# Weight splits of an up-projection asked for one step earlier, and rows of x loaded one by one

## The chip, the core and the metric

The kernel runs on one core of a Trainium2 chip. TensorE (PE) does the matrix products, ScalarE (ACT), VectorE (DVE) and GpSimd (POOL) work beside it, and SyncE (SP) asks for most of the DMA transfers. The metric is the device time of one execution in microseconds (us), as a median of several. Three runs before the change gave 2205.82, 2207.04 and 2207.34 us.

## The reference

One layer of a hybrid encoder works on 2048 prompt tokens and 64 sample tokens of 1024 channels. The first half (normalised input, a combined projection, a pooling mixer, a chunked matrix memory, an output projection) is not touched by the change. The second half is a gated MLP with a causal convolution of width 3 over the tokens:

```python
h2 = rmsnorm(x, g2) * (1 + sc2) + sh2
up = h2 @ w_up                                   # 1024 -> 2 * 2816
upp = jnp.concatenate([conv_buf, up], 1)
conv = b_conv + sum(w_conv[j] * upp[:, j:j + T] for j in range(3))
a, g = jnp.split(conv, 2, -1)
x = x + gt2 * ((jax.nn.silu(g) * a) @ w_down)    # 2816 -> 1024
y = rmsnorm(x, g_final)
```

All of it is f32, and the products have to be as exact as three passes make them: each operand is kept as a high half (rounded to the type that PE multiplies) and a low half (what is left), and a product is high times high, high times low and low times high.

## The kernel before the change

**Groups, parts, pairs.** The MLP works on the 2112 tokens in three groups (`o.g` 0, 1, 2) of 704 tokens each. The 22 pairs of column blocks of `w_up` (block f of `a` and block f of `g`, 128 columns each) are taken in parts: 5, 5, 6 and 6 pairs in groups 0 and 1, and 6, 4, 4, 4 and 4 in group 2. Behind each part stands a down part, which multiplies the part's results with rows of `w_down` and adds them to the rows of x.

**Products.** A pair's two column blocks are computed by a scheme of Winograd's kind: seven products in place of eight, each of 12 matmuls of 352 columns (4 blocks of the inner dimension, 3 passes), with sums of weights and sums of inputs prepared earlier. `Pair.products` (the part of the code around L1575 to L1650) emits in this order: B11, B21, then the last product T4 of the pair before, then T2, T3, B22 and T1. The function `product` (L1539) emits one of them: it calls `pump()`, takes a weight unit with `get_unit()`, and emits its 12 matmuls (L1546). Between two products stand steps on ACT and DVE for this pair and the pair before, called in the program `rest(...)`:

- `copy_u4` (L1625, ACT) copies the sum left by T1 from PSUM, and `sum_g1` and `sum_a` (L1555, DVE) add it to two others.
- `self.s1` (L1593, ACT) is copied after B11, and `ea` (L1605, DVE) is its sum with B21's result. It reads the PSUM bank in which B22 later starts, so B22 has to wait for it. `sum_g0` is `eg` at L1555.
- `scale_a` and `scale_g` (L1529, ACT; tiles `ta` and `tg`) begin the convolution, `taps_a` and `taps_g` (L1534, DVE) finish it. Then come `silu` (L1656, ACT), `gate` (L1663, DVE) and the split of the result into halves `av` (L1682, ACT, and L1692, DVE).

**Weight units.** All weights come through one stream of units in the order of their use. A unit of `w_up` or `w_down` is loaded into a `raw` tile (L368, four of them) and split into a `wt` tile (six of them, taken in turn): the high half by ACT (L384), then the low half by DVE (L387). A unit of sums (`wsum`, L376) is loaded straight into a `wt` tile and split there; a unit that was split and stored by group 0 (`wsplit`, L373) is loaded whole and needs no split. In groups 1 and 2 a pair takes three raw units (for B11, B21 and T4), two of sums (for T3 and B22) and two whole ones (for T2 and T1); in group 0 four are of sums, and two of these are stored with L392. The unit for B22 is called the B22 sum below, the one for T3 the T3 sum.

**pump.** `pump()` looks at the first four units that wait for their use: it emits both halves of the split for the first three and only ACT's high half for the fourth. Then it asks for loads while fewer than seven units wait and fewer than six `wt` tiles are in use (`live[0]`), and `product` takes one from that count after its matmuls. So a unit's high half stands on ACT three products ahead of its use, and its low half on DVE two products ahead.

**What sets the order.** On PE, ACT, DVE and POOL the order is the one in which the program emits (a manual schedule). On SP a scheduler sets the order of the DMA requests; SP works them off one after the other, and a request that waits for a free tile holds up those behind it.

**Rows of x.** In the last step of a down part, `down_end` (L2072), the result of each of the eight rows is added to a row of x, which `load_x2` (L1867) fetches. In group 0 two rows are asked for after each pair. In group 1 three rows are asked for after the last pair of the first part, and the other five in one go before that part's down part (L2037). In group 2 the rows come another way.

Of the kernel before, what the change touches and what calls it, by code (L numbers as in the profile page):

```python
# [18 lines left out]
KD = D // P  # L19
# [9 lines left out]
NE = 3  # L29
# [33 lines left out]
def tile_layer(ctx: ExitStack, tc: tile.TileContext, xT, vecs, cst, rst, rowv, w_mod, w_ada, w_qkou, w_v, w_pool,  # L63
# [12 lines left out]
    def bank(nm, shape=(P, 512)):  # L76
        q = turn[nm]
        q.append(q.pop(0))
        return q[-1].tile(list(shape), F32, tag="bank", name=nm)
# [3 lines left out]
    def mm_ps():  # L83
        return bank("mm")
# [18 lines left out]
    def tick(i=0):  # L103
        q = bg[i]
        while q:
            try:
                next(q[0])
                return
            except StopIteration:
                q.pop(0)  # L110
# [130 lines left out]
    for g in range(NG):  # L241
        o = Grp()
# [118 lines left out]
    def issue():  # L361
        u = Unit()
        src, u.n, place, u.keep, u.stays = stream[pos[0]] + (OUT, None, False)[len(stream[pos[0]]) - 2:]
        u.at = pos[0]
        if place == OUT:
            u.raw = raw_tile()
            to = u.raw[:, :u.n]
            nc.sync.dma_start(out=to if len(src.shape) == 2 else to.rearrange("p (s c) -> p s c", s=2), in_=src)  # L368
        else:
            u.w = wt_tile(u.n)  # L370
            if place == WHOLE:
                u.state = 2
                nc.sync.dma_start(out=u.w.bitcast(F32)[:, :, :u.n], in_=src)  # L373
            else:
                u.raw = u.w.bitcast(F32)[:, 1]
                nc.sync.dma_start(out=u.raw[:, :u.n], in_=src)  # L376
        pos[0] += 1
        pend.append(u)

    def work_out(u, upto=2):  # L380
        if u.state == 0 and upto > 0:
            if u.w is None:
                u.w = u.home()
            act.activation(u.w[:, 0, :u.n], u.raw[:, :u.n], AF.Copy)  # L384
            u.state = 1
        if u.state == 1 and upto > 1:
            dve.tensor_tensor(out=u.w[:, 1, :u.n], in0=u.raw[:, :u.n], in1=u.w[:, 0, :u.n].bitcast(F32), op=ALU.subtract)  # L387
            u.state = 2
# [5 lines left out]
    def pump():  # L394

        while True:
            for i, u in enumerate(pend[:ahead[1]]):
                if u.w is not None or live[0] < ahead[2] or u.stays:
                    work_out(u, 2 if i < ahead[1] - ahead[3] else 1)
            if (pos[0] >= len(stream) or len(pend) >= ahead[0] or live[0] >= ahead[2]  # L400
                    or sum(u.w is None for u in pend) >= RB
                    or pos[0] < n_att and sum(u.w is not None for u in pend) >= WB - 2):
                break
            issue()

    def get_unit():
        if not pend:
            issue()
        u = pend.pop(0)
        work_out(u)  # L410
        keep(u)
        return u.w
# [218 lines left out]
    for g in range(NFG):  # L631
        o = Grp()
# [868 lines left out]
    def do(n=1):  # L1501

        for _ in range(n):
            if todo:
                todo.pop(0)()

    def both_of(a, b):
        return lambda: (a(), b())
# [32 lines left out]
    def product(ps, Bo, nm, first):  # L1541
        pump()
        U = get_unit()
        for kc in range(4):
            for pi, (a, b) in enumerate(PASSES):
                pe.matmul(ps[:, :FH], U[:, a, kc * P:(kc + 1) * P], Bo.at(nm, kc, b),  # L1546
                          start=(first and kc == 0 and pi == 0), stop=(kc == 3 and pi == 2), skip_group_check=not first)
            if kc % 2:
                tick(0)
        tick(5)  # L1550
        live[0] -= 1

    def plus(o, half, ext, u, ps):
        for (a, b, d) in spans(o, half):
            dve.tensor_tensor(out=ext[:, d:d + b - a], in0=ps[:, a:b], in1=u[:, a:b], op=ALU.add)  # L1555
# [4 lines left out]
    class Pair:  # L1560
# [10 lines left out]
        def products(self, old):  # L1571
# [12 lines left out]
            def extra(i):  # L1584
                for at, step in self.more:
                    if at == i:
                        step()
            rest((old, Pair.copy_u4), (older, Pair.gate))
            product(b1, Bo, "B11", True)
            rest((old, Pair.sum_g1), (old, Pair.sum_a))  # L1590
            extra(0)
            self.s1 = half_tile("s1")
            act.activation(self.s1, b1[:, :FH], AF.Copy)  # L1593
            rest((older, Pair.split_hi))
            product(b2, Bo, "B21", True)
            rest((old, Pair.scale_a), (older, Pair.split_lo))
            extra(1)
# [263 lines left out]
    def load_x2(o, ks=range(KD)):  # L1861
        x3 = []
        for k in ks:
            if k % 2 == 0:
                xp[k // 2] = f2.tile([P, 2 * FT], F32, tag=f"x{k}", name=f"x{k}")
            x = xp[k // 2][:, k % 2 * FT:(k % 2 + 1) * FT]
            got = nc.sync.dma_start(out=x, in_=x2d[k, :, o.t0:o.t0 + FT])  # L1867
            if o.g > 0:
                tc.keep_in_program_order(got)
            x3.append(x)  # L1870
        return x3
# [90 lines left out]
    x3, ssum = [], None  # L1962
    act.activation(RF[:, 0:1], V[:, 0:1], AF.Silu)
    bg[5].append(down_sums())
    for o in fgroups:
# [5 lines left out]
        for pi, (f0, f1_) in enumerate(SPARTS if o.g in SGS else PARTS):  # L1971
# [46 lines left out]
            if o.g in SGS and pi == 0:  # L2018
                Y = [f2.tile([P, 2 * FT], F32, tag=f"x{2 * m}", name=f"x{2 * m}") for m in range(4)]
                x3 = [Y[n // 2][:, n % 2 * FT:(n % 2 + 1) * FT] for n in range(KD)]  # L2020
            if o.g in SGS and not lastp:
# [11 lines left out]
                do(9)  # L2033
                held.append(pair)
                continue
            if pi == 0 and o.g > 0:
                x3 += load_x2(o, range(len(x3), KD))  # L2037
            if not o.last:
                if lastp:
                    drain(0, 1)  # L2040
# [7 lines left out]
            def down(ps, W, ks, secs, stays=False):  # L2048
                for k in ks:
                    U = W.at(k // 4)  # L2050
                    for (a, b) in PASSES:
                        for i, (lo, hi) in enumerate(secs):
                            pe.matmul(ps[i][:, :hi - lo], U[:, a, k % 4 * P:(k % 4 + 1) * P], av[k](b, lo, hi),  # L2053
                                      start=(k == 0 and (a, b) == PASSES[0]), stop=(k == nf - 1 and (a, b) == PASSES[-1]))
                    if (k % 4 == 3 or k == nf - 1) and not stays:
                        live[0] -= 1
                    pump()
                    if todo:
                        do()
                    elif o.last:  # L2060
                        tick(1 - k % 2)
                    else:
                        tick((1, 5, 5, 5)[k % 4])

            def down_end(n, ps, secs):
                while Y and n not in made:
                    next(conv)
                for i, (lo, hi) in enumerate(secs):
                    for (a, b, s) in o.segs:
                        a, b = max(a, lo), min(b, hi)  # L2070
                        if a < b:
                            dve.scalar_tensor_tensor(out=x3[n][:, a:b], in0=ps[i][:, a - lo:b - lo], scalar=gt2(n, s),  # L2072
                                                     in1=x3[n][:, a:b], op0=ALU.mult, op1=ALU.add)
                if not lastp:
                    return
                lo, hi = secs[0][0], secs[-1][1]
                if ends and n == KD - 1:
                    sq7 = fscr()
                    act.activation(sq7[:, :hi - lo], x3[n][:, lo:hi], AF.Square)
                    sums.append((sq7, lo))  # L2080
                else:
                    fsq_acc(ssum, x3[n][:, lo:hi], lo, hi, n == 0)
                if ends:
                    act.activation(x3[n][:, lo:hi], x3[n][:, lo:hi], AF.Copy, scale=V[:, V_GF + n:V_GF + n + 1])
# [7 lines left out]
            todo.extend([both_of(pair.sum_g1, old.gate), both_of(pair.sum_a, old.split_hi), both_of(old.split_lo, pair.scale_a)])  # L2092
            for n in range(NE - 1):
                pss.append([mm_ps() for _ in both])
                down(pss[n], Ws[n], range(nf - 2), both)
                if n == 0:
                    do(9)
                    pair.last_product()
                    todo.extend([both_of(pair.sum_g0, pair.scale_g), pair.taps_a, pair.taps_g, pair.silu, pair.gate,
                                 pair.split_hi, pair.split_lo])  # L2100
            for n in range(NE - 1):
                down(pss[n], Ws[n], [nf - 2], both)
            pss.append([mm_ps() for _ in both])
            down(pss[-1], Ws[-1], range(nf - 1), both)
            do(9)
            for n in range(NE):
                down(pss[n], Ws[n], [nf - 1], both)
# [2 lines left out]
            for secs in [(c,) for c in ENDS] if ends else (both,):  # L2110
                sums = [(ssum, 0)]
                for n in range(NE, KD):
                    ps = [mm_ps() for _ in secs]
                    down(ps, rows[n], range(nf), secs, ends)
                    down_end(n, ps, secs)
                if ends:
                    bg[0].append(final_end(o, x3, sums, *secs[0]))
        if not o.last:
            drain(1)
            bg[0].append(final(o, x3, ssum))  # L2120
            x3 = []
# [86 lines left out]
```

## Time and profile before

| what | value |
|---|---|
| median of three runs | 2207.04 us |
| the profiled execution's own time | 2208.67 us |
| its span in the profile | 2206.9 us |
| granted TensorE clock, mean | 0.998 |
| DVE busy | 1660.9 us, 75% of the span |
| ACT busy | 1037.7 us, 47% |
| DMA moved | 521.66 MB, mean 236 GB/s |

The profile page gives the busy time of each engine and groups of instructions by line, with the idle time of their engine just before them and what ended it. PEld is the weight load of TensorE, which runs ahead of the matmuls; its idle time is the better measure of a wait, because a matmul's end in the profile is modelled. The timeline gives instructions in order of time, equal neighbours merged into one row: start, duration, engine, line, what is written from what, how many, and in square brackets the idle time before and who ended it. "SPq" is SP's queue of requests, where the duration of a merged row reaches from the first request to the end of the last.

### The profile page before, as it was taken

What the parts mean: (1) busy time and instruction counts of PE and PEld (TensorE: products, weight loads), DVE (VectorE), ACT (ScalarE), POOL (GpSimd) and SP (SyncE); (2) the same over time, 40 slices, a digit from 0 to 9 for tenths busy, and PEclk for the clock granted to TensorE, in tenths of its full rate; (3) what the DMA queues carried; (4) which work ended last, traced back from release to release, by engine and by line L of the source; (5) the groups of instructions that cost most, each with busy time, mean ns of one, the idle gap of its engine ahead of it and who ended that gap; (6) DMA issues with size and microseconds to landing.
All of it is one profiled execution on the core that took longest, in us unless ns stands there. A gap on an engine that the chain in (4) does not pass through costs nothing. (4 is left out here: it accounts for less than half of the span.)

```text
span 2206.9 us, 38374 instructions
## 1 busy us (share of the span) xinstructions
PE 2180.6 (99%) x13708; PEld 2067.8 (94%) x13708; DVE 1660.9 (75%) x3124; ACT 1037.7 (47%) x2024; POOL 224.3 (10%) x514
## 2 busy tenths in 40 slices
PE   8999999999999999999999999999999999999998
PEld 7888888888899999999999999999999999999998
DVE  5887669577765778797958687787857597888885
ACT  4653334235243456464636444545435355555454
POOL 0010000001000100000101210000000321011112
PEclk9999999999999999999999999999999999999999
DMA  9977987997898696768667975667468665555562
GB/s 348 363 246 261 336 276 241 324 325 242 282 331 275 223 310 200 233 207 275 212 197 234 308 235 192 218 193 245 152 203 255 204 198 168 159 162 179 160 199 81
DMA packets 294975, 521.66 MB, mean 236 GB/s; under 512 B 26456, under 2 KB 115928, under 8 KB 294784
## 3 DMA queue, kind: packets, MB, share of 16 engines
q1 hardware_dynamic: 280448, 482.74, 67.2%
q10 hardware_dynamic: 11776, 28.09, 3.3%
q0 software_dynamic: 2560, 8.39, 1.0%
q8 instruction: 108, 1.77, 0.3%
q14 instruction: 83, 0.68, 0.1%
HBM read 399.97 MB, written 119.14 MB: 235 GB/s over the span
## 5 line engine op out<-in xcount | busy, mean ns | idle before, releaser
L1546 PE MATMUL mm<-hx,wt 128*128 128x352 f32 x5544 | 893.0, 322 | 5.3 <-DVE wt L387 3.7
L1546 PEld LDWEIGHTS mm<-hx,wt 128*128 128x128 f32 x5544 | 880.5, 188 | 13.1 <-DVE wt L387 9.1
L441 PE MATMUL mm<-hl,wt 128*128 128x512 f32 (+2 forms) x1920 | 395.8, 358 | 2.1 <-DMA wt<-hl_kept 2.1
L2053 PE MATMUL mm<-av,wt 128*128 128x352 f32 (+2 forms) x2400 | 386.9, 322 | 2.1 <-ACT av L1682 1.8
L2053 PEld LDWEIGHTS mm<-av,wt 128*128 128x128 f32 x2400 | 382.2, 188 | 4.3 <-ACT av L1682 2.1
L384 ACT ACTIVATE wt<-raw 128x512 fp32r<-128x512 f32 (+3 forms) x510 | 288.3, 579 | 207.3 <-PE mm L2053 60.9
L387 DVE TENSOR_TENSOR wt<-raw,wt 128x512 fp32r<-128x512 f32 (+3 forms) x510 | 323.4, 648 | 65.8 <-ACT wt L384 65.3
L441 PEld LDWEIGHTS mm<-hl,wt 128*128 128x128 f32 x1920 | 312.5, 188 | 49.6 <-issue 5.3
L441 PE MATMUL mm<-mx,wt 128*128 128x512 f32 (+1 forms) x960 | 186.5, 353 | 0.0
L441 PEld LDWEIGHTS mm<-mx,wt 128*128 128x128 f32 x960 | 158.7, 188 | 25.1 <-ACT mx L1402 1.1
L384 ACT ACTIVATE wt<-wt 128x512 fp32r<-128x512 f32 x176 | 110.3, 627 | 108.3 <-DMA wt<-wsum 101.3
L1534 DVE SCALAR_TENSOR_TENSOR tg<-eg,V,tg 128x704 f32<-128x704 f32 (+1 forms) x132 | 125.7, 952 | 33.6 <-ACT tg L1529 31.3
L387 DVE TENSOR_TENSOR wt<-wt 128x512 fp32r<-128x512 f32 x176 | 119.5, 686 | 31.0 <-ACT wt L384 30.9
L2072 DVE SCALAR_TENSOR_TENSOR x<-mm,MOD,x 128x352 f32<-128x352 f32 (+4 forms) x152 | 77.9, 559 | 75.2 <-PE mm L2053 75.2
L1534 DVE SCALAR_TENSOR_TENSOR ta<-ea,V,ta 128x704 f32<-128x704 f32 (+1 forms) x132 | 125.5, 950 | 5.9 <-ACT ta L1529 3.5
L1801 PE MATMUL mm<-av,wt 128*128 128x352 f32 x576 | 95.5, 322 | 0.0
L1801 PEld LDWEIGHTS mm<-av,wt 128*128 128x128 f32 x576 | 92.8, 188 | 0.0
L1610 ACT ACTIVATE u<-mm 128x352 f32<-128x352 f32 x66 | 30.5, 462 | 120.4 <-PE mm L1546 58.0
L206 DVE SCALAR_TENSOR_TENSOR acc<-raw,CA,acc 128x512 f32<-128x512 f32 x84 | 60.5, 745 | 32.4 <-DMA raw<-w_ada 32.3
L1656 ACT ACTIVATE tg<-tg 128x704 f32<-128x704 f32 (+1 forms) x66 | 52.3, 793 | 63.8 <-DVE tg L1534 63.7
L1555 DVE TENSOR_TENSOR eg<-mm,u 128x352 f32<-128x352 f32 x154 | 69.8, 465 | 13.2 <-ACT u L1625 9.6
L1138 PE MATMUL mm<-wt,hl 128*128 128x256 f32 (+1 forms) x576 | 70.9, 282 | 0.0
(332 smaller groups left out, 2282.7 us busy)
## 6 DMA issues: line engine op xcount, KB each, us to landing
wt<-hl_kept SPq DMA_DIRECT2D x108, 512.0 KB, 6.0
raw<-w_up SPq DMA_DIRECT2D x198, 256.0 KB, 3.9
wt<-wsum SPq DMA_DIRECT2D x176, 256.0 KB, 4.5
wt<-wsplit SPq DMA_DIRECT2D x88, 512.0 KB, 4.5
w<-w_up SPq DMA_DIRECT2D x88, 256.0 KB, 5.6
wsum<-w SPq DMA_DIRECT2D x44, 512.0 KB, 5.8
wsplit<-wt SPq DMA_DIRECT2D x44, 512.0 KB, 5.5
raw<-w_down SPq DMA_DIRECT2D x88, 256.0 KB, 4.2
```

Source lines behind the costliest of these rows:

```text
L206: dve.scalar_tensor_tensor(out=acc[s], in0=w, scalar=CA[:, k, s:s + 1], in1=acc[s], op0=ALU.mult, op1=ALU.add)
L384: act.activation(u.w[:, 0, :u.n], u.raw[:, :u.n], AF.Copy)
L387: dve.tensor_tensor(out=u.w[:, 1, :u.n], in0=u.raw[:, :u.n], in1=u.w[:, 0, :u.n].bitcast(F32), op=ALU.subtract)
L441: pe.matmul(ps[bi][:, :hi - lo], U[:, a, k % 4 * P:(k % 4 + 1) * P], mv[k][:, b, lo:hi], start=(at == 0 and pi == 0), stop=(k == order[-1] ...
L1138: pe.matmul(ps[ti][:n, :cols], h[4 * kh + k4][:, b, lo:lo + n], U[:, a, k4 % 2 * cols:(k4 % 2 + 1) * cols], start=(kh == 0 and k4 == 0 and ...
L1534: dve.scalar_tensor_tensor(out=t[:, :E], in0=ext[:, j:j + E], scalar=wc(j, f), in1=t[:, :E], op0=ALU.mult, op1=ALU.add)
L1546: pe.matmul(ps[:, :FH], U[:, a, kc * P:(kc + 1) * P], Bo.at(nm, kc, b), start=(first and kc == 0 and pi == 0), stop=(kc == 3 and pi == 2), ...
L1555: dve.tensor_tensor(out=ext[:, d:d + b - a], in0=ps[:, a:b], in1=u[:, a:b], op=ALU.add)
L1656: act.activation(self.tg[:, :E], self.tg[:, :E], AF.Silu)
L1801: pe.matmul(ps, U[:, x, w:w + P], quad.d[nm][z], start=(start and k == 0 and pi == 0), stop=(k == 1 and pi == 2), skip_group_check=not start)
L2053: pe.matmul(ps[i][:, :hi - lo], U[:, a, k % 4 * P:(k % 4 + 1) * P], av[k](b, lo, hi), start=(k == 0 and (a, b) == PASSES[0]), stop=(k == n ...
L2072: dve.scalar_tensor_tensor(out=x3[n][:, a:b], in0=ps[i][:, a - lo:b - lo], scalar=gt2(n, s), in1=x3[n][:, a:b], op0=ALU.mult, op1=ALU.add)
```

## The change

```diff
@@ product
                 tick(0)
         tick(5)
         live[0] -= 1
+        pump()
@@ the loop over groups and parts, ahead of the down part
-            if pi == 0 and o.g > 0:
-                x3 += load_x2(o, range(len(x3), KD))
+            def row(n):
+                if len(x3) <= n < KD:
+                    x3.extend(load_x2(o, range(len(x3), n + 1)))
@@ the down part (NE is 3, KD is 8)
                 pss.append([mm_ps() for _ in both])
+                row(n)
                 down(pss[n], Ws[n], range(nf - 2), both)
...
             pss.append([mm_ps() for _ in both])
+            row(NE - 1)
             down(pss[-1], Ws[-1], range(nf - 1), both)
+            row(NE)
             do(9)
...
                     ps = [mm_ps() for _ in secs]
+                    row(n + 1)
                     down(ps, rows[n], range(nf), secs, ends)
```

The first part adds a call of `pump()` behind each product. The call at the head of the next product then finds nothing left to do, so the splits and requests of one `pump()` move ahead of the steps that stand between two products. Nothing is added or taken away on PE, ACT or DVE, and PE's own order is unchanged; up to the MLP, SP's order is unchanged too. Line numbers after L1551 move by one, those after L2036 by two or more.

The second part asks for a row of x one step before it is needed. It reaches one place, the first down part of group 1, where five rows were asked for at once.

**Place 1: ACT and DVE between two pairs of group 1 (pair 18 handing over to pair 19).** In these rows `wt_18145` and `wt_18143` are the T3 sum, `wt_18183` and `wt_18178` the B22 sum, `wt_18273` and `wt_18267` the B11 weights of pair 20, `wt_18295` and `wt_18293` its B21 weights. ACT before:

```order
L1625 ACTIVATE u4_18179<-mm_18032 128x352
L1593 ACTIVATE s1_18201<-mm_18177 128x352
L1682 ACTIVATE av_18203<-tg_18121 128x352 x2
L384 ACTIVATE wt_18145<-wt_18145 128x512
L1529 ACTIVATE ta_18222<-ea_18099,V_105 128x704
L384 ACTIVATE wt_18183<-wt_18183 128x512
L1610 ACTIVATE u2_18267<-mm_18177 128x352
L1529 ACTIVATE tg_18270<-eg_18197,V_105 128x704
L384 ACTIVATE wt_18273<-raw_18228 128x512
L384 ACTIVATE wt_18295<-raw_18230 128x512
```

ACT after:

```order
L1626 ACTIVATE u4_18182<-mm_18035 128x352
L384 ACTIVATE wt_18143<-wt_18143 128x512
L1594 ACTIVATE s1_18204<-mm_18180 128x352
L1683 ACTIVATE av_18206<-tg_18125 128x352 x2
L384 ACTIVATE wt_18178<-wt_18178 128x512
L1529 ACTIVATE ta_18228<-ea_18102,V_105 128x704
L384 ACTIVATE wt_18267<-raw_18223 128x512
L1611 ACTIVATE u2_18271<-mm_18180 128x352
L1529 ACTIVATE tg_18274<-eg_18200,V_105 128x704
L384 ACTIVATE wt_18293<-raw_18225 128x512
```

Each high half has moved ahead of the steps between two products: the B22 sum's now stands ahead of the scaling `ta`, behind which it stood.

DVE before, the same stretch (`dq` is background work on sums of `w_down`):

```order
L387 TENSOR_TENSOR wt_18145<-wt_18145 128x512
L1534 SCALAR_TENSOR_TENSOR ta_18222<-ea_18099,V_105,ta_18222 128x704 x2
L1605 TENSOR_TENSOR ea_18246<-mm_18178,s1_18201 128x352
L1555 TENSOR_TENSOR eg_18197<-mm_18123,u2_18118 128x352
L387 TENSOR_TENSOR wt_18183<-wt_18183 128x512
L1780 TENSOR_TENSOR dq_18175<-dq_18175 128x128
L1781 TENSOR_TENSOR dq_18175<-dq_18175 128x128
L1783 TENSOR_TENSOR dq_18175<-dq_18175 128x128
L1784 TENSOR_TENSOR dq_18175<-dq_18175 128x128
L1534 SCALAR_TENSOR_TENSOR tg_18270<-eg_18197,V_105,tg_18270 128x704 x2
L387 TENSOR_TENSOR wt_18273<-raw_18228,wt_18273 128x512
L387 TENSOR_TENSOR wt_18295<-raw_18230,wt_18295 128x512
```

DVE after:

```order
L387 TENSOR_TENSOR wt_18178<-wt_18178 128x512
L1534 SCALAR_TENSOR_TENSOR ta_18228<-ea_18102,V_105,ta_18228 128x704 x2
L1606 TENSOR_TENSOR ea_18249<-mm_18181,s1_18204 128x352
L1556 TENSOR_TENSOR eg_18200<-mm_18127,u2_18122 128x352
L1781 TENSOR_TENSOR dq_18175<-dq_18175 128x128
L1782 TENSOR_TENSOR dq_18175<-dq_18175 128x128
L1784 TENSOR_TENSOR dq_18175<-dq_18175 128x128
L1785 TENSOR_TENSOR dq_18175<-dq_18175 128x128
L387 TENSOR_TENSOR wt_18267<-raw_18223,wt_18267 128x512
L1534 SCALAR_TENSOR_TENSOR tg_18274<-eg_18200,V_105,tg_18274 128x704 x2
L387 TENSOR_TENSOR wt_18293<-raw_18225,wt_18293 128x512
L387 TENSOR_TENSOR wt_18312<-raw_18245,wt_18312 128x512
```

The low half of the B22 sum stood behind the two sums `ea` and `eg` and now stands ahead of the taps `ta`; of the next pair's three raw low halves, one now stands ahead of the taps `tg` and two behind them.

**Place 2: SP, the request for the B22 sum of pair 20 in group 1.** Here `wt_18297` and `wt_18295` are the T3 sum of that pair, `wt_18333` and `wt_18328` its B22 sum. SP before:

```order
L373 DMA wt_18275<-wsplit_130 128x1024
L376 DMA wt_18297<-wsum_129 128x512
L368 DMA raw_18378<-w_up 128x512
L368 DMA raw_18399<-w_up 128x512
L376 DMA wt_18333<-wsum_129 128x512
```

SP after:

```order
L373 DMA wt_18269<-wsplit_130 128x1024
L368 DMA raw_18374<-w_up 128x512
L376 DMA wt_18295<-wsum_129 128x512
L368 DMA raw_18393<-w_up 128x512
L368 DMA raw_18515<-w_down 128x512
L376 DMA wt_18328<-wsum_129 128x512
```

Two raw requests still stand right ahead of the B22 sum, one unit further on in the stream than before. With four raw tiles, `raw_18393` and `raw_18515` take the tiles of `raw_18225` and `raw_18245`, so they wait for the two low halves that stand last in DVE's rows above, behind the taps `tg`.

**Place 3: SP around the first down part of group 1.** `raw_14813` before and `raw_14802` after are the same unit, the third piece of 128 columns of `w_down`; the tiles x2, x4 and x6 take rows 3 to 7 of x. SP before:

```order
L368 DMA raw_14767<-w_down 128x128
L368 DMA raw_14785<-w_down 128x128
L1867 DMA x2_14639<-x2d_132 128x704
L1867 DMA x4_14800<-x2d_132 128x704 x2
L1867 DMA x6_14803<-x2d_132 128x704 x2
L368 DMA raw_14813<-w_down 128x128
L368 DMA raw_14824<-w_down 128x512
```

SP after:

```order
L368 DMA raw_14757<-w_down 128x128
L368 DMA raw_14784<-w_down 128x128
L368 DMA raw_14802<-w_down 128x128
L1868 DMA x2_14642<-x2d_132 128x704
L1868 DMA x4_14805<-x2d_132 128x704 x2
L368 DMA raw_14821<-w_down 128x512
```

The third 128-column piece now stands ahead of the rows of x, and three rows stand there in place of five; rows 6 and 7 come later, among the first requests for the next part's `w_up`.

## The prediction, made before the changed kernel was run

> **What bounds the kernel now.** I read the page's busy times first, then the waits of TensorE, then the timeline of a quiet pair.
>
> ```profile
> span 2206.9 us, 38374 instructions
> PE 2180.6 (99%) x13708; PEld 2067.8 (94%) x13708; DVE 1660.9 (75%) x3124; ACT 1037.7 (47%) x2024; POOL 224.3 (10%) x514
> L1546 PEld LDWEIGHTS mm<-hx,wt 128*128 128x128 f32 x5544 | 880.5, 188 | 13.1 <-DVE wt L387 9.1
> PEld mm L1546 <- DVE wt L387: 9.1, 19, 0.7
> PEld mm L2053 <- ACT av L1682: 2.1, 1, 2.1
> ```
>
> PE is busy 99% of the span, and the change takes no matmul away. So it can win only what PE idles: 13.1 us in the 462 products, 9.1 us of it in 19 waits for the low half of a weight, and one wait of 2.1 us in a down part. It can lose much more, because every step between two products stands in an in-order queue that PE needs within a few us. The rhythm shows in a quiet stretch of group 1. ACT's timeline of pair 19:
>
> ```profile
> 1652.79 0.46 ACT L1625 ACTIVATE u<-mm 128x352 f32<-128x352 f32 x1 [1.01 <-PE mm L1546]
> 1654.69 0.46 ACT L1593 ACTIVATE s<-mm 128x352 f32<-128x352 f32 x1 [1.44 <-PE mm L1546]
> 1655.82 0.62 ACT L384 ACTIVATE wt<-wt 128x512 fp32r<-128x512 f32 x1
> 1656.34 0.97 ACT L1529 ACTIVATE ta<-ea,V 128x704 f32<-128x704 f32 x1
> 1658.16 0.63 ACT L384 ACTIVATE wt<-wt 128x512 fp32r<-128x512 f32 x1 [0.85 <-DMA wt<-wsum]
> 1660.48 0.47 ACT L1610 ACTIVATE u<-mm 128x352 f32<-128x352 f32 x1 [1.69 <-DVE eg L1555]
> 1660.84 0.97 ACT L1529 ACTIVATE tg<-eg,V 128x704 f32<-128x704 f32 x1
> 1666.09 0.47 ACT L1625 ACTIVATE u<-mm 128x352 f32<-128x352 f32 x1 [0.74 <-PE mm L1546]
> ```
>
> The copies at 1652.79 and 1666.09 each wait for the end of a T1, so a pair takes 13.30 us, 1.90 us for each of seven products. B22 is the sixth: PE reaches it 9.50 us after the first copy, at 1662.29 by this clock. The row at 1658.16 is the high half of the B22 sum. It waited 0.85 us for its load, behind the scaling `ta`, where the wait cost nothing.
>
> **The change part by part.**
>
> *Rows of x.* These rows are SP's, ACT's and PE's (weight load) in the first down part of group 1, and the windows around it:
>
> ```profile
> 1335.75 0.93 SPq L368 DMA_DIRECT2D raw<-w_down  x2
> 1336.73 2.52 SPq L1867 DMA_DIRECT2D x<-x2d  x5
> 1339.35 0.85 SPq L368 DMA_DIRECT2D raw<-w_down  x2
> ...
> 1342.33 0.29 ACT L384 ACTIVATE wt<-raw 128x128 fp32r<-128x128 f32 x1
> 1347.02 0.31 ACT L384 ACTIVATE wt<-raw 128x128 fp32r<-128x128 f32 x1 [4.39 <-DMA raw<-w_down]
> 1347.23 0.96 ACT L1529 ACTIVATE tg<-eg,V 128x704 f32<-128x704 f32 x1
> 1352.02 0.79 ACT L1682 ACTIVATE av<-tg 128x704 fp32r<-128x704 f32 x1 [0.44 <-DVE tg L1663]
> ...
> 1352.86 0.30 PEld L2053 LDWEIGHTS mm<-av,wt 128*128 128x128 f32 x2 [2.06 <-ACT av L1682]
> 1353.79 0.50 PEld L2053 LDWEIGHTS mm<-av,wt 128*128 128x128 f32 x2 [0.63 <-DVE av L1692]
> ...
> 1340.00:1350.00 10.00, 10.00 (x65) 10.00 (x65) 6.44 (x10) 3.04 (x5) 0.31 (x2) 1.00 0.57 184
> 1350.00:1360.00 10.00, 7.89 (x39) 7.31 (x39) 7.26 (x15) 3.76 (x7) 0.00 (x0) 0.83 0.19 48
> 1354.00:1356.00 2.00, 2.00 (x7) 2.00 (x8) 1.26 (x3) 0.31 (x1) 0.00 (x0) 0.50 0.20 38
> ```
>
> Five rows of x went ahead of the third 128-column piece, asked for at 1339.35. ACT stood 4.39 us for it at 1347.02, with `tg` behind, and PE waited 2.06 and 0.63 us for the last `av`. The window then holds 39 matmuls where the one before holds 65: 26 x 0.154 us = 4.0 us lost, since the granted clock fell to 0.50 right behind the wait. After the change the piece is asked for at about 1336.7 and has until 1342.6, 5.9 us, where the whole delay was 7.7 us with five rows in front. I take the stall as gone: **-4.0 us** (bounds 0 and -4.0). Late next is `av`, at 1352.02 - 4.39 = 1347.6 at the earliest, against the wait that ended at 1352.86 and began 2.06 us earlier: 3 us to spare. Rows 6 and 7 now come among the next part's requests; if one is late, a sum on DVE waits, not PE, as three sets of two PSUM banks turn. The Trainium skill ("TensorE: Matmul & The Clock Gate", section "What's actually happening") lets the clock fall only after an idle window of about 3.4 us. By that rule this edit would give 2.7 us, the two waits alone; the row of 0.50 says otherwise.
>
> *Low halves earlier.* A typical stall, DVE's rows and PE's:
>
> ```profile
> 2124.34 0.53 DVE L1605 TENSOR_TENSOR ea<-mm,s 128x352 f32<-128x352 f32 x1
> 2125.21 1.07 DVE L1848 SCALAR_TENSOR_TENSOR x<-x,MOD,fscr 128x640 f32<-128x640 f32 x2
> 2126.20 0.69 DVE L387 TENSOR_TENSOR wt<-wt 128x512 fp32r<-128x512 f32 x1
> ...
> 2126.93 1.38 PE L1546 MATMUL mm<-hx,wt 128*128 128x352 f32 x7 [0.39 <-DVE wt L387]
> ```
>
> The low half of the B22 sum stands behind `ea`, `eg` and background work; it now goes ahead of the taps and these sums. PE then waits for `ea`, one low half (0.69 us) later than before: at 2124.87 + 0.69 = 2125.56 here, before PE needs it. Where no background work stands between, as in the quiet pair's rows further down, the low half ends at 1660.96 and `ea` at 1659.94; with `ea` 0.69 later, only 0.3 of a 0.7 us stall goes. Of 9.1 us I take **-5 us**, about midway (bounds 0 and -9.1).
>
> *High halves earlier.* The T3 sum's high half goes ahead of `s1`, which idles 1.44 us for PE anyway; the B11 weights' goes ahead of `u2`, which waits 1.69 us for DVE. Both cover 0.6 us, and uncovered they would cost that much. The B22 sum's high half goes ahead of `ta`, and that is not covered: its load can't start earlier, because its tile comes free with T1, so `ta` now waits for the transfer. The other views of the same pair, DVE and SP, and the landing of such loads:
>
> ```profile
> 1657.34 1.94 DVE L1534 SCALAR_TENSOR_TENSOR ta<-ea,V,ta 128x704 f32<-128x704 f32 x2 [0.17 <-ACT ta L1529]
> 1659.41 0.53 DVE L1605 TENSOR_TENSOR ea<-mm,s 128x352 f32<-128x352 f32 x1
> 1660.28 0.68 DVE L387 TENSOR_TENSOR wt<-wt 128x512 fp32r<-128x512 f32 x1
> 1662.07 1.93 DVE L1534 SCALAR_TENSOR_TENSOR tg<-eg,V,tg 128x704 f32<-128x704 f32 x2
> 1663.92 1.29 DVE L387 TENSOR_TENSOR wt<-raw,wt 128x512 fp32r<-128x512 f32 x2
> ...
> 1652.78 0.33 SPq L376 DMA_DIRECT2D wt<-wsum  x1
> 1664.63 0.94 SPq L368 DMA_DIRECT2D raw<-w_up  x2
> 1666.08 0.33 SPq L376 DMA_DIRECT2D wt<-wsum  x1
> ...
> wt<-wsum SPq DMA_DIRECT2D x176, 256.0 KB, 4.5
> DMA to landing us min/median/max: 2.9/4.5/7.6
>   ACT wt L384: 101.3, 78
> ```
>
> The load asked for at 1652.78 landed at 1658.16. From the landing on, each with its distance in the rows: high half to `ta` 0.52 (1655.82 to 1656.34); `ta` to its taps 1.00 (to 1657.34); to `ea` 2.07 (to 1659.41); on to `tg` 1.43 (to 1660.84); `tg` to its taps 1.00, as for `ta`; to the two raw low halves 1.85 (1662.07 to 1663.92); both done 1.29; two requests on SP about 0.4 more. Sum 9.56 us. Then SP may ask for the next pair's B22 sum, because in the new order two raw requests that need just these low halves stand ahead of it. That closes a loop: with the median landing of 4.5 us a turn takes 14.06 us, and PE's pair 13.30. Before, the loop was open: `ta` needed no load, the raw requests were out at 1664.63 to 1665.57, and the B22 sum's at 1666.08 waited for PE alone.
>
> What a pair has in hand: asked for at 0, landed at 4.5, `ea` ends 0.52 + 1.00 + 2.07 + 0.53 = 4.12 later, at 8.62, due at 9.50. So a part's second pair (the first has no older pair) has 0.88 us to spare, the third 0.12, and from the fourth PE loses 0.76 us each. By SP's new order, two such requests, or one of them, stand ahead of the B22 sum in 35 pairs from the third of a part on, 12 of which are the first so placed; 23 x 0.76 = **+17.5 us**. Bounds: with landings of 3.7 us and less the turn fits into 13.30 and it costs nothing; with 4.9 us each turn loses 1.16 and a part's third pair 0.68 already, 23 x 1.16 + 12 x 0.68 = 35 us. I take the median: the quiet pair's 5.4 us and the least, 2.9 us, lie on both sides of it. The Trainium skill ("DMA: Bandwidth & Descriptors", section "Rules for kernel authors") says to issue a DMA early and wait for it late. The change does half of it: the wait moves up, the request can't; the 78 waits of 101.3 us show that most of these waits are real already.
>
> POOL's requests keep their places, and the down parts' splits stood behind each block already: nothing there.
>
> **Sum.** -4.0 - 5 + 17.5 = +8.5 us on the span of 2206.9. The profiled execution took 2208.67 us, 1.63 above the median of the runs; the median 2207.04 becomes 2215.5.
>
> **The rivals.** *The loop stays open* (faster): loads of these sums land in 3.7 us or less in most pairs, so the 1.44 to 1.69 us of idle ACT time take the wait, and the two gains stand: 2207.0 - 4 - 5 = 2198, or 2194 with all 9.1 us. For it: the least landing is 2.9 us. Against it: the median of 4.5. It decides at 3.74 us (13.30 - 9.56). *Gain and loss cancel* (no difference): landings near 4.2 us lose 0.46 a turn, 23 x 0.46 = 10.6 us, and background work that already holds DVE up hides a part; 2203 to 2211. *The rows of x do nothing*: the piece is still late because three rows follow it on the same rings; then 2219.5, inside the range.
>
> **How the numbers follow.** The slower case has 0.58: the wait for the load ahead of `ta` is certain, and only its size is open. No difference has 0.22, faster 0.20. A measurement of this kernel tells about 0.2% (4.4 us) from no change. The time is the likeliest case's, 2215.5. The low end, 2199, leaves out the better half of the faster case; the high end, 2233, is that of landings of 4.9 us (2207 + 35 - 9).
>
> **What would show it.** Right: `ta` on ACT starts about 0.5 us behind a high half that waited for `wt<-wsum`; new waits of L1546 for `DVE ea L1606` in the fourth and later pairs of a part; the B22 sum's request later than the end of T1 by up to 1.5 us; and the window after 1350 with 65 matmuls. Wrong: no waits for `ea`, with the landing of these loads below 3.7 us; or the PE idle time of L1546 below 9 us.

## The result: 57 us slower, and the profile after

The changed kernel takes 2263.59 us (median of 4 runs, 2263.39 to 2268.3), beside 2206.43 us for the kernel before in the same session (2204.88 to 2207.34). The ratio is 1.0265, with a 95% interval of 1.0247 to 1.0283. The forecast had the right sign and the wrong size: it said +8.5 us, at most +26, and it is +57.

The changed kernel's page, its first lines and the rows of the up-projection's matmuls and weight loads (busy time, mean ns, idle time before them and what ended most of it):

```profile
span 2261.7 us, 38449 instructions
PE 2194.2 (97%) x13708; PEld 2072.4 (92%) x13708; DVE 1663.1 (74%) x3124; ACT 1036.5 (46%) x2024; POOL 229.5 (10%) x514
...
L1546 PE MATMUL mm<-hx,wt 128*128 128x352 f32 x5544 | 907.5, 324 | 47.8 <-DVE ea L1606 28.7
L1546 PEld LDWEIGHTS mm<-hx,wt 128*128 128x128 f32 x5544 | 886.9, 189 | 64.0 <-issue 35.1
```

All engines are as busy as before to within 14 us; only PE's idle time in the 462 products has grown, from 13.1 to 64.0 us in its weight loads. The changed kernel's view of waits says for what (us in total, times, longest):

```profile
PEld mm L1546 <- issue: 35.1, 32, 2.5
PE mm L1546 <- DVE ea L1606: 28.7, 27, 2.2
PEld mm L1546 <- ACT s L1594: 15.9, 9, 4.2
PEld mm L1546 <- DVE eg L1556: 9.2, 15, 1.7
PEld mm L1546 <- DVE wt L387: 1.0, 2, 0.6
ACT wt L384 <- DMA wt<-wsum: 197.1, 111, 5.2
```

The last two rows answer to rows shown of before: the waits for low halves have gone from 9.1 us to 1.0, and ACT's waits for the sums' loads have doubled, from 101.3 us to 197.1. The first four are new or were near nothing. (The weight load's 32 gaps put down to "issue" are mostly the matmuls' waits for `ea`: it has its weights, but the matmul ahead of it stands.) The wait of 2.06 us for `av` in the down part is gone.

The order of PE's work is the same in both kernels, so its products can be laid side by side, one by one. For each product I took how much longer the gap ahead of it is than before, and how much longer it lasts itself, and summed by kind. This is worked out from PE's rows of both traces, and the table is used for the experiments too ("late" is the longer gap ahead of a product; "downs" is the same for the gap from a part's last product, a T4, to the next part's first, and from the very last one to PE's end; "start" is the shift at which the first product begins):

```
us against before        late B22 late T2 late T4 downs  B11 longer  other longer  start   sum
changed kernel               33.7    13.5     8.9  -5.0     -3.8         7.4       -0.2   54.5
```

Three kinds of late products make 56 us: **B22** in 32 of the 53 pairs that have an older pair in their part, **T2** in the parts' first pairs, and **T4**. The forecast had only the first, with 17.5 us.

### The profile page after: what moved, and what is told of

The parts are those of the page before. It is cut to its first block, busy times and chain, and to the rows that moved or that the text cites. A ratio compares the mean times of both kernels' runs of the same rounds, so it can differ in the third digit from the quotient of the medians.

```text
span 2261.7 us, 38449 instructions
## 1 busy us (share of the span) xinstructions
PE 2194.2 (97%) x13708; PEld 2072.4 (92%) x13708; DVE 1663.1 (74%) x3124; ACT 1036.5 (46%) x2024; POOL 229.5 (10%) x514
## 5 line engine op out<-in xcount | busy, mean ns | idle before, releaser
L1546 PE MATMUL mm<-hx,wt 128*128 128x352 f32 x5544 | 907.5, 324 | 47.8 <-DVE ea L1606 28.7
L384 ACT ACTIVATE wt<-wt 128x512 fp32r<-128x512 f32 x176 | 110.6, 629 | 227.8 <-DMA wt<-wsum 197.1
L206 DVE SCALAR_TENSOR_TENSOR acc<-raw,CA,acc 128x512 f32<-128x512 f32 x84 | 60.4, 744 | 30.7 <-DMA raw<-w_ada 30.7
```

The lines of the kernel that those rows point to most:

```text
L206: dve.scalar_tensor_tensor(out=acc[s], in0=w, scalar=CA[:, k, s:s + 1], in1=acc[s], op0=ALU.mult, op1=ALU.add)
```

## Where the time stands in the trace

The third pair of group 2's fourth part begins at 2084.14 (its first B11). ACT, DVE, SP and PE of the changed kernel there:

```profile
2084.67 0.45 ACT L1626 ACTIVATE u<-mm 128x352 f32<-128x352 f32 x1
2086.61 0.44 ACT L1594 ACTIVATE s<-mm 128x352 f32<-128x352 f32 x1
2090.49 0.63 ACT L384 ACTIVATE wt<-wt 128x512 fp32r<-128x512 f32 x1 [3.44 <-DMA wt<-wsum]
2091.02 0.96 ACT L1529 ACTIVATE ta<-ea,V 128x706 f32<-128x706 f32 x1
...
2091.15 0.69 DVE L387 TENSOR_TENSOR wt<-wt 128x512 fp32r<-128x512 f32 x1 [3.56 <-ACT wt L384]
2092.02 1.94 DVE L1534 SCALAR_TENSOR_TENSOR ta<-ea,V,ta 128x706 f32<-128x706 f32 x2 [0.18 <-ACT ta L1529]
2094.10 0.53 DVE L1606 TENSOR_TENSOR ea<-mm,s 128x352 f32<-128x352 f32 x1
2096.51 1.94 DVE L1534 SCALAR_TENSOR_TENSOR tg<-eg,V,tg 128x706 f32<-128x706 f32 x2 [0.42 <-ACT tg L1529]
2098.37 1.29 DVE L387 TENSOR_TENSOR wt<-raw,wt 128x512 fp32r<-128x512 f32 x2
...
2085.64 0.37 SPq L376 DMA_DIRECT2D wt<-wsum  x1
2099.09 0.33 SPq L368 DMA_DIRECT2D raw<-w_up  x1
2099.69 0.37 SPq L368 DMA_DIRECT2D raw<-dsum  x1
2100.16 0.41 SPq L376 DMA_DIRECT2D wt<-wsum  x1
...
2094.77 7.54 PE L1546 MATMUL mm<-hx,wt 128*128 128x352 f32 x45 [0.96 <-DVE ea L1606]
```

This is the forecast's loop, step for step. The B22 sum is asked for at 2085.64, 1.50 us after the pair's begin, because SP stood for raw tiles. It lands at 2090.49. ACT has stood 3.44 us for it ahead of `ta`, and DVE 3.56 us for the high half ahead of the taps. `ea` ends at 2094.63, 4.14 us after the landing (forecast 4.12), and B22 has waited 0.96 us for it. The two raw low halves end at 2099.66, and the next pair's B22 sum is asked for at 2100.16, 9.67 us after the landing (forecast 9.56). The turn is 9.67 + 4.85 = 14.5 us long, against PE's 13.30. This pair is a usual one: over the 32 requests that came late in a part's third pair or a later one, the way to the request from the high half one pair earlier has a median of 9.7 us (9.3 to 11.1).

The first pair of a part was not in the forecast. ACT and SP in the first pair of group 0's second part, whose B11 begins at 915.31, and PE's windows (columns: length, PE busy and its matmuls, granted clock, DMA share, GB/s):

```profile
915.39 0.63 ACT L384 ACTIVATE wt<-wt 128x512 fp32r<-128x512 f32 x1 [3.09 <-DMA wt<-wsum]
922.18 0.63 ACT L384 ACTIVATE wt<-wt 128x512 fp32r<-128x512 f32 x1 [6.15 <-DMA Bd<-fscr]
922.71 0.45 ACT L1594 ACTIVATE s<-mm 128x352 f32<-128x352 f32 x1
...
914.56 1.74 SPq L376 DMA_DIRECT2D wt<-wsum  x2
...
914.00:918.00 4.00, 4.00 (x27) 1.00 1.01 374
918.00:922.00 4.00, 1.28 (x9) 0.97 1.03 406
922.00:924.00 2.00, 0.79 (x3) 0.50 0.71 273
924.00:926.00 2.00, 2.00 (x8) 0.50 0.33 133
926.00:928.00 2.00, 2.00 (x8) 0.50 0.92 263
```

The row at 922.18 is the B22 sum's high half, and the copy `s1`, which T2 needs, stands behind it. The load was asked for at 914.56 and landed 7.6 us later. (The row names a transfer of `Bd`, which ended near that time; the landing of the sum is what this instruction reads.) In the kernel before, where this B11 begins at 908.01, ACT has the two in the other order:

```profile
910.11 0.46 ACT L1593 ACTIVATE s<-mm 128x352 f32<-128x352 f32 x1 [1.14 <-PE mm L1546]
914.52 0.63 ACT L384 ACTIVATE wt<-wt 128x512 fp32r<-128x512 f32 x1 [3.95 <-DMA wt<-wsum]
```

There the load took 7.3 us from request to high half, nearly as long, and `s1` did not pay for it. In the changed kernel PE was busy for 2.07 of the 6 us from 918 on, so it stood for 3.9 us, and then it ran at half the clock: 8 matmuls in 2 us beside 27 in 4 us.

## The experiments

In each, the comparison is with the kernel before, run in turns on the same chip.

**1 and 2. The two parts apart.** Rows of x alone (the pump at the product's end taken out), and the pump alone.

```
# rows_only                        # ends_only (the kernel before, and)
         live[0] -= 1                       live[0] -= 1
-        pump()                   +        pump()
```

> Only the rows of x are loaded one by one; weights are split and asked for as before the change. Theory (the whole loss is in the up-projection's order): PE's gaps from a part's last T4 to the next part's first B11 shrink as in the changed kernel, by 4.1 us in group 1's first down part and 1.3 us in group 2's, so about 2201 us beside 2206.5 before. Rival (rows that come late hold up the sums behind the down part): 2207 or more.

> Splits and loads at the products' ends, rows of x in one go as before. Theory: the changed kernel's 2263.6 without the 5.4 us that the rows save, so 2269. Rival (rows cost): below 2263.

The rows alone took 2205.32 us beside 2207.5, ratio 0.999 (0.9981 to 0.9999), where 2201 was expected. The ends alone took 2261.61, ratio 1.0244 (1.0227 to 1.0262). So the whole loss comes with the pump at the ends, and the rows cost nothing. The window of the stall, in the trace with the rows alone:

```profile
1340.00:1350.00 10.00, 10.00 (x65) 1.00 0.57 180
1350.00:1360.00 10.00, 10.00 (x65) 1.00 0.17 49
```

It holds 65 matmuls where before it held 39. But the sum "rows -5.4, so 2269 without them" failed: with the ends alone the gaps between the products shrank by 5.4 us too, and the time was below 2263, the rival's number, though the rows cost nothing in the run beside it. The ends ask for the late piece of `w_down` ahead of the rows, so either part removes that stall, and they don't add up.

**3 and 4. What in the ends costs: the order of one split, or the earlier requests?**

```
# b22_high_behind_ta               # loads_at_ends
-    def pump():                   -    def pump():
+    def pump(most=9):             +    def pump(split=True, load=True):
-    enumerate(pend[:ahead[1]])    -    enumerate(pend[:ahead[1]])
+    enumerate(pend[:min(most,     +    enumerate(pend[:ahead[1]]
+                   ahead[1])])    +              if split else [])
...                                ...
-        pump()                    -        pump()
+        pump(3 if nm == "B21"     +        pump(split=False)
+             else 9)
```

> The changed kernel, with one high half per pair (that of the B22 sum) put back behind the scaling ta; its requests stay at the products' ends, and DVE's order stays as it is in the changed kernel. Theory (ta waits for that landing and hands the wait to B22): the 33.7 us by which B22's starts lie later go, so 2230, and PE's waits for ea vanish (below 3 us, against 28.7). Rival (requests made earlier crowd each other and land later, whatever stands ahead of ta): 2255 or more, with the waits moved to the low half or the load of B22.

> The changed kernel, but a product's end only asks for loads; splits stay at the next product's begin, as before the change. Theory (the order of the splits costs all of it): 2198 to 2205, the rows' 5.4 us gained and the earlier requests worth little. Rival (the earlier requests cost): above 2230.

The first took 2259.14 us, ratio 1.0228 (1.0205 to 1.0251): the theory expected 2230 and failed as it stood; the number is the rival's (2255 or more), which the runs 5 and 6 below decide against. The second took 2232.82, ratio 1.0111 (1.0094 to 1.0128), above the 2198 to 2205 of the theory and again where its rival (the earlier requests cost) had put it. ACT's `ta` and DVE in the kernel with the high half behind `ta`, in the same pair as above:

```profile
2080.53 0.98 ACT L1529 ACTIVATE ta<-ea,V 128x706 f32<-128x706 f32 x1 [0.16 <-DVE ea L1556]
...
2084.16 0.69 DVE L387 TENSOR_TENSOR wt<-wt 128x512 fp32r<-128x512 f32 x1 [3.12 <-ACT wt L384]
2084.77 1.94 DVE L1534 SCALAR_TENSOR_TENSOR ta<-ea,V,ta 128x706 f32<-128x706 f32 x2
2086.84 0.53 DVE L1606 TENSOR_TENSOR ea<-mm,s 128x352 f32<-128x352 f32 x1
```

`ta` was done 3 us before, but the low half of the same sum stands ahead of the taps on DVE, and it waits 3.12 us for the landing just so. From the landing, the way over DVE (0.66 to the low half, 0.61 to the taps) is only 0.2 to 0.3 us shorter than the way over ACT. The loop has two entrances, and closing one leaves the other. The forecast had counted this low half among the gains.

The loads alone lose in another way: B22's late starts are gone (0.7 us), but T4 runs 16.6 us longer in all, waiting inside for low halves (57 waits, 30.7 us):

```profile
PEld mm L1546 <- DVE wt L387: 30.7, 57, 1.9
```

A raw unit needs one of the six weight tiles to be split into, and by the code a load asked for earlier takes that tile first. I read that in the code and did not try it apart. This kernel therefore doesn't tell what the early requests cost in the changed kernel, where the splits go ahead with them.

**5 to 8. The B22 sum as the whole cause.** The new theory: the split of this one sum, moved ahead on ACT and on DVE and in the first pairs ahead of `s1`, makes nearly all of the loss.

```
# b22_both_halves_behind (with pump(most) as above)
+        pump({"B21": 3, "T4": 2}.get(nm, 9))
# b22_sum_left: the units of the B22 sums are noted in a set, b22
+    def pump(leave=()):
+                if u.at not in leave and (u.w is not None
+                        or live[0] < ahead[2] or u.stays):
...
+        pump(b22)
# no_end_of_T1                     # b22_sum_left_no_end_of_T1
+        nm in ("T1",) or pump()   +        nm == "T1" or pump(b22)
```

> The changed kernel, with the B22 sum's high half behind the scaling ta and its low half behind ea, so that neither ACT nor DVE stands for that landing between a part's second and last pair; all other splits, and all requests, at the products' ends. Theory (the low half ahead of the taps closes the loop by itself, which is why moving the high half alone won 4 us): B22's late starts, 28 to 36 us in three kernels, fall below 5 us, so about 2232. The first pairs' waits for s1 and the waits of T4 stay. Rival (the early requests cost): 2250 or more.

> The changed kernel, but the B22 sum is split only where it was before the change, in the first pair of a part too; all other splits, and all requests, at the products' ends. Theory (nearly the whole loss is this one sum): of 2263.6 go 33.7 us of late B22 starts, 13.5 us of late T2 starts in the parts' first pairs and some 5 us by which T2 and T3 then run longer, so 2211. Rival 1 (T2's wait goes on to T3, whose weights are late as well): about 2225. Rival 2 (requests): above 2240.

> The changed kernel without the splits and requests at the end of T1; they come at B11's begin, behind the copy u4, as before the change. Theory (a raw high half stands ahead of u4, and two low halves ahead of the sums behind it): T4's late starts, 8.9 us, go, the rest stays: 2255. Rival (T4 waits for the background work that also stands on ACT and DVE there): 2260 or more.

> Both edits at once: the B22 sum split where it was before the change, and nothing asked for at the end of T1. Theory: none of the three new waits is left, and the gains are (5.4 us by the rows, some 4 us of weights' low halves that come in time): 2199 to 2203, below the kernel before. Rival (the low halves' gain comes from the end of T1 too): 2205 or more.

Measured: both halves behind, 2217.78 us, ratio 1.0042 (1.0028 to 1.0056); the sum left where it was, 2210.33, ratio 1.0015 (1.0005 to 1.0024); without T1's end, 2241.51, ratio 1.0152 (1.0136 to 1.0168); both edits, 2210.17, ratio 1.0014 (1.0002 to 1.0026). The table of products:

```
us against before        late B22 late T2 late T4 downs  B11 longer  other longer  start   sum
rows_only                     0.0     0.2    -0.5  -4.9      0.7         1.3        2.2   -1.0
b22_high_behind_ta           27.4    13.2     9.1  -3.7     -3.7         5.9        1.7   50.0
b22_both_halves_behind       -0.3    13.2     2.4  -5.2     -3.7         1.0        1.2    8.7
b22_sum_left                  0.5     0.1     4.1  -5.1     -3.8         2.7        0.8   -0.8
no_end_of_T1                 15.2    12.3     8.1  -5.4     -3.7         2.5        4.8   33.8
```

With both halves behind, B22's late starts are gone, 33.7 us to -0.3, and with them most of T4's and of what products last longer: the loop was worth 46 us of time, not 34. With the sum left in the first pairs too, T2's 13.5 us go as well, and the time is the theory's 2211. So 53 of the 57 us hang on where one sum is split, with every other split and every request still at the products' ends. The wait did not pass on from T2 to T3, and requests that go out at the ends together with the other splits cost little.

Both edits together were expected below the kernel before, at 2199 to 2203; the 2210 us are the rival's. T4 still starts 4.0 us late there (5.2 us in group 0, a little early elsewhere), as with the sum left alone; no run settles why.

The theory of T1's end fell. T4's late starts stayed (8.1 us); what went is half of B22's. In the last pairs of group 2's parts T4 starts 0.8 to 1.2 us late in the changed kernel and not at all once the B22 sum is left alone, so those are the loop's tail; what stays of T4 then, 4.1 us, is group 0's. That B22's late starts fell from 33.7 to 15.2 goes with earlier requests (0.7 us behind B11's begin on average over the 53 pairs, against 1.0) and shorter landings: from the request to the high half it takes 4.3 us on average, against 4.6. Fewer requests for raw weights go out in the 2.5 us ahead of the sum's (1.0 a pair, against 1.5); that this shortens the landing is argued, not shown.

**9 and 10. Is the sum enough by itself, and is it a loop?**

```
# b22_sum_early_alone (rows_only, and at the product's end)
+        [work_out(u, 2 if i < 3 else 1)
+         for i, u in enumerate(pend[:4]) if u.at in b22]
# b22_asked_by_ACT (the changed kernel, and in issue())
-                nc.sync.dma_start(out=u.raw[:, :u.n], in_=src)
+                (act if u.at in b22 else nc.sync).dma_start(out=u.raw[:, :u.n], in_=src)
```

> The kernel before the change, with the rows of x one by one as in the changed kernel, and of the rest of the change only this: the B22 sum is split at the products' ends (its high half ahead of ta, in a part's first pair ahead of s1; its low half ahead of the taps). No other split and no request moves in the code. Theory (this one sum is enough): late B22 and T2 starts as in the changed kernel, 33.7 and 13.5 us, and some 5 us of longer T2 and T3, on 2205: about 2257. Rival (it takes the other splits and requests too, since they decide when SP asks): below 2235.

> The changed kernel, but the load of the B22 sum is asked for on ACT's queue, just ahead of the copy u4, which waits for the end of T1 too; so it doesn't stand on SP behind the raw requests. The order of the splits stays. Theory (the loop: the request comes 1.5 us late because SP stands for low halves that wait, over ta and tg, for the last landing): asked for 0.2 to 0.5 us after B11's start in every pair, PE loses only what a landing exceeds 5.0 us by, 8 to 10 us in all instead of 33.7; with the first pairs' waits as they are, 2236 to 2241. Rival (no loop; ta pays for each landing by itself): B22's late starts stay above 25 us, 2255 or more.

The sum alone, split early, took 2276.51 us, ratio 1.0325 (1.0303 to 1.0346): more than the whole change, and above the 2257 of the theory. Late B22, T2 and T4 are 28.5, 13.3 and 8.7 us, near those of the changed kernel (33.7, 13.5 and 8.9); the larger difference is B11, which runs 10.3 us longer here and 3.8 us shorter there. So the sum is enough, and the other early low halves give some of it back.

With the request on ACT's queue it took 2245.85 us, ratio 1.0193 (1.0175 to 1.0211), between the theory's 2241 and the rival's 2255. ACT in one pair of group 2 of that kernel:

```profile
2082.94 0.33 ACTq L376 DMA_DIRECT2D wt<-wsum  x1
2083.32 0.47 ACT L1626 ACTIVATE u<-mm 128x352 f32<-128x352 f32 x1 [0.92 <-PE mm L1546]
2083.83 0.63 ACT L384 ACTIVATE wt<-wt 128x512 fp32r<-128x512 f32 x1
2087.41 0.63 ACT L384 ACTIVATE wt<-wt 128x512 fp32r<-128x512 f32 x1 [1.92 <-DMA wt<-wsum]
2087.95 0.96 ACT L1529 ACTIVATE ta<-ea,V 128x706 f32<-128x706 f32 x1
```

The request goes out as T1 ends, 0.2 us after B11's begin, and `ta` still stands behind the landing, but B22 is no longer late. In groups 1 and 2 the late B22 starts fell from 22.2 us to 9.0, in all from 33.7 to 20.2. About half of what is left is long landings: 6.8 us in one pair and 6.0 in another gave 1.8 and 1.0 us, the excess over 5.0. The other half is three pairs of group 1 whose request was late all the same, by 1.0 to 2.7 us. That is the loop broken open with the order of the splits unchanged, if not in every pair. In group 0 it failed, 11.2 us as before, since the request stands on ACT behind another high half there; that is why the time is 2246 and not below 2241.

**11 and 12. A version that beats both?** Ends of T3 and B22 alone, with the rows, and the rows alone once more.

```
# ends_of_T3_and_B22
+        nm in ("T3", "B22") and pump()
```

> Rows of x one by one, and splits and requests at the ends of T3 and B22 alone, where the B22 sum's are already done. Theory (B11's raw low halves, now ahead of the taps of tg, come in time, and nothing waits for a landing): the 3.7 us that B11 runs shorter in the changed kernel, on top of the rows' 2 to 5 us: 2198 to 2203, faster than before by 0.2 to 0.4%. Rival (the taps of tg come later, and gate and av with them): 2205 or more.

> Rows of x one by one, nothing else of the change, once more with more rounds: the one part that gained. The trace of the first such run shows 5 us less between the products, its times only 2.2 us less. Theory (the 5 us are there, and what else differed, the start of the MLP and products of group 0, is scatter): ratio 0.998 to 0.999. Rival (the later rows give it back elsewhere, in the products that follow): ratio 1.000, with the same products longer again.

The ends of T3 and B22 took 2214.4 us, ratio 1.0043 (1.0029 to 1.0056): the rival. B11 runs 3.7 us shorter, but T4 starts 8.0 us late, waiting for `eg`:

```profile
PEld mm L1546 <- DVE eg L1556: 9.5, 13, 1.6
```

On DVE, a raw low half stands ahead of the taps of `tg` there, and the sums `eg` come after. The rows alone took 2205.43 us beside 2207.51, ratio 0.9991 (0.998 to 1.0002), after 0.999 the first time. They are the only part that is not slower, and what they win, about 2 us, is at the edge of what can be told. The 5 us in the gaps are in both traces; the MLP began 2 us later in both, which nothing in it explains.

## Why the prediction was right in sign and wrong in size

The forecast was +8.5 us and the two traces differ by 54.5, 46.0 us more. Of these, 18.7 us are a step that it costed at nothing (the high half ahead of `s1` in the parts' first pairs), 16.2 us a term that it mis-sized (the loop), 8.9 us late T4 starts, which it did not have, and 2.2 us other products that last longer. The gains came as summed, 9.0 us (downs, B11 and start together).

- **Rows of x, -4.0 us.** Right in the trace: -4.1 us in that down part and -1.3 us in group 2's, the window at 65 matmuls, the clock at 1.00. It is not a gain of its own beside the ends, which remove the same stall.
- **Low halves earlier, -5 us.** Right in size: the waits fell from 9.1 to 1.0 us, and B11 runs 3.8 us shorter. Wrong in one of these halves: the B22 sum's, of which the text said that `ea` comes one low half later "before PE needs it". It carries the landing's whole wait to the taps and to `ea`, and closes the loop without ACT's help.
- **The loop, +17.5 us (bounds 0 and 35).** The mechanism is the one that was forecast, to 0.1 us in its steps, and it is mis-sized. It lost 33.7 us in B22's late starts, in 32 pairs where 23 were counted, 1.05 us each where 0.76 was taken. The count failed because it let the loop begin in a part's fourth pair: 10.7 us fell in 11 second and third pairs. One median landing for all hid these: the high half came 6.9 us after the request in group 0's first part, and the second pair was late already. From the fourth pair on 23.0 us were lost in 21 pairs, 1.10 us each. From the request to the high half it took 4.76 us there on average, where 4.5 was taken, and from there to the next request 9.7, where 9.56 was summed; by these figures a turn should lose 1.16 us (estimate). And the late pairs made T4 late behind them, so that undoing the loop won 46 us.
- **High halves earlier, costed at nothing.** This is the step that failed outright. The text took the sum that goes ahead of `s1` for T3's, whose load has landed. That holds in pairs with an older pair. A part's first pair has no T4, so the fourth unit there is the B22 sum, asked for at the end of the down part. In eight of the 13 parts it landed only 3.6 to 6.9 us after B11's begin. T2 waited for `s1` behind it, 13.5 us in all, and T2 and T3 ran another 5.2 us longer, 4.4 of it in two pairs in which the granted clock behind the wait was 0.50 to 0.62. The forecast said that uncovered this half would cost 0.6 us, its own length: it costs the wait for its load.
- **What would show it.** All four signs came: `ta` 0.53 us behind a high half that waited for its load, the waits for `ea` (in second and third pairs too), the late request, and, with the rows alone, the window with 65 matmuls. Of the 40 pairs from a part's third on, 32 had a late request, 1.5 us behind B11's begin on average and 2.9 at most, beside 0.2 where it was in time; the forecast had said up to 1.5. The signs were there at twice the loop's price, so the signs alone did not test the sum.
- **The range.** Its high end took the loop's upper bound and the gains in full, but nothing for the steps costed at zero, and T2's wait with what follows it made some 19 us, late T4 starts another 9. The low end, 2199, was said to leave out the better half of the faster case; at 2194 to 2198 it left out all of it.

## What to carry to other kernels

An instruction that is moved ahead in an in-order queue brings its wait with it, and everything behind it then pays for the landing; its own duration says nothing of the cost. Follow such a move on every engine that handles the same data (here the high half on ACT and the low half on DVE), and through the irregular first and last rounds, where the unit at that place in the queue is another one. Where a wait ahead feeds back into the next request, price it over the spread of the landings too, which decides in which round the loop begins, and not by their median alone.

## What the runs showed of the hardware

The clock fell behind short waits of PE, and not behind every one. PE's windows of the changed kernel around a late B22 of group 0, which waited 2.20 us for `ea`, and behind a T2 of group 1 that had waited 1.81 us for `s1` until 1405.30:

```profile
866.00:870.00 4.00, 1.80 (x12) 1.00 0.24 94
870.00:873.00 3.00, 3.00 (x12) 0.60 0.47 167
873.00:876.00 3.00, 3.00 (x17) 0.83 0.16 50
...
1406.00:1408.00 2.00, 2.00 (x10) 0.62 1.02 397
1408.00:1410.00 2.00, 2.00 (x9) 0.53 0.75 290
```

Behind the first wait the granted clock was 0.60 for 3 us, and the next two products lasted 1.7 us longer in all: nearly as much again as the wait. Behind the second the next two lasted 1.7 us longer as well. Two other waits of B22 in the same trace, of 1.9 us each, cost 0.1 us beyond themselves. The Trainium skill ("TensorE: Matmul & The Clock Gate", section "What's actually happening") has the clock fall after an idle window of about 3.4 us; here 2.2 and 1.8 us were enough, and by that rule the 1.7 us would not have been lost either time.
